# The state space branch by blocks of eight tokens: three matrices for each channel tile and a scan over 64 blocks

## The chip, the core and the metric

The kernel runs on one core of a Trainium2 chip. The metric is the time that the device measures for one execution, in microseconds (us). TensorE (PE in the rows) multiplies matrices and writes PSUM. VectorE (DVE), ScalarE (ACT) and GpSimd (POOL) work on tiles of 128 partitions. SyncE (SP) issues the DMAs of this kernel, in the order in which they stand in its queue. Every engine works through its own queue in order; an instruction that waits holds up those behind it.

## The reference, cut to what matters

The program is two layers of a first block (convolution, latent attention, a recurrent branch) and one layer of a second block. The second block has a differential attention with 8 heads, a state space branch (S5) over 1024 channels, and a merge of both. S5 has 64 groups of 16 channels, each group with 64 complex states; 512 tokens go through it one after the other:

```python
def s5_branch(u, lam_re, lam_im, log_dt, b_re, b_im, c_re, c_im, d_skip, w_glu, b_glu):
    ...
    mag = jnp.exp(lr * dt)
    ab_re = mag * jnp.cos(li * dt)
    ab_im = mag * jnp.sin(li * dt)
    ...
    bu_re = jnp.einsum('bsgc,gpc->bsgp', uf, bb_re)
    bu_im = jnp.einsum('bsgc,gpc->bsgp', uf, bb_im)
    ...
    _, _, xs_re, xs_im = lax.associative_scan(combine, (a_re, a_im, bu_re, bu_im), axis=1)
    y = (jnp.einsum('bsgp,gcp->bsgc', xs_re, c_re.astype(f32))
         - jnp.einsum('bsgp,gcp->bsgc', xs_im, c_im.astype(f32)))
    y = y.reshape(bsz, seq, D_SSM) + d_skip.astype(f32) * u.astype(f32)
    y = jax.nn.gelu(y.astype(u.dtype))
    return y * jax.nn.sigmoid(y @ w_glu + b_glu)
```

So the state is x(t) = a x(t-1) + B u(t) with a complex a per state, and the output is Re(C x(t)) + d u(t).

## The kernel before

Activations lie with 128 channels on the partitions and 512 tokens along the row. Each large product with a weight is made of three matmuls over 128x512 (`mm3`, lines 184 to 186: high by high, high by low, low by high parts). A weight comes in as 128 x 1024 raw values (`load_w`, line 159), ScalarE rounds it to the high part (line 169), VectorE subtracts for the low part (line 170). There are two raw buffers and three buffers each of high and low parts.

The second block runs over eight turns q = 0 to 7 (`second_block`). A turn does channel tile q of S5 (`ssm_u`, then `ssm_tile`), head q of the attention's scores (`diff_scores`), head q-1 of its values (`diff_values`) and a gate; its six input projections are 6 x 48 = 288 of the three-part matmuls. I call such a turn a head.

In `ssm_tile` four pairs of groups (128 complex states each) follow one another. Two matmuls give B u (line 1527). Four VectorE products with a cosine and a sine table (1529 to 1533) and two GpSimd sums (1531, 1534) turn every token's input back by its angle, so that two real scans over 512 tokens with the decay alone (1536, 1537) give the states; three VectorE products, two VectorE sums and two GpSimd products (1538 to 1543) turn them forward again; eight matmuls with C, 32 output columns each (1551), close the tile. The tables are read from DRAM (`CS`, 512 KB for a pair).

The tables are made in the output projections of layers 0 and 1 of the first block. `out_proj` runs over 16 column tiles c; after each it takes one more piece of a generator `k.prep`: first `ssm_prep` (parameters, B and C matrices), then `rotations` (32 tables; 10 in layer 0 and 22 in layer 1). In layer 1 `out_proj` also keeps three weighted sums on VectorE (1156, 1158) and two on GpSimd (1153, 1154).

The order of each engine's queue is set by a scheduler that simulates the program as written; weight loads have a high priority. Line numbers of the changed kernel are smaller by one to three in the unchanged part.

## Time and profile before

| what | value |
|---|---|
| median of 3 runs | 3424.55 us (3423.64 to 3424.78) |
| the profiled execution, and its span | 3426.18 us, span 3424.4 us |
| TensorE busy | 3306.3 us (97%) |
| VectorE busy | 1995.6 us (58%) |
| ScalarE, GpSimd busy | 1191.6 us (35%), 860.8 us (25%) |
| mean granted clock of TensorE | 0.981 |

The span is divided by the profile into 40 slices of 85.6 us; counted from 1: slices 24 to 31 are heads, slices 21 and 22 lie in the output projection of layer 1. Busy time of TensorE counts a matmul from its start to its modelled end, and matmuls overlap, so a busy share near 1 doesn't say that TensorE issues as fast as it can. How many matmuls start in a stretch says more.

### The profile page before, as it was taken

The page shows a single profiled execution, that of the slowest core. Times are in us where ns is not written, and L with a number is a line of the kernel's source. Part 1 is how long each engine was busy: PE and PEld are TensorE (multiplying, and loading weights), DVE is VectorE, ACT ScalarE, POOL GpSimd, SP SyncE. Part 2 cuts the span into 40 slices and gives each one's busy share as a digit, 9 for nine tenths or more (in the row PEclk, how much of TensorE's full clock was granted, in tenths as well). Part 3 has the DMA queues.
Part 4 walks back from the last instruction along what each step waited for, and adds up shares of the span by engine and source line. Part 5 has one row for each costly group of instructions (what it writes and reads, how often), then busy time and mean ns, then how long its engine had stood idle before and what let it go on. Part 6 is the DMA issues. An engine that isn't in the chain of part 4 may idle for free.

```text
span 3424.4 us, 41918 instructions
## 1 busy us (share of the span) xinstructions
PE 3306.3 (97%) x15603; PEld 2666.6 (78%) x15603; DVE 1995.6 (58%) x3035; ACT 1191.6 (35%) x1950; POOL 860.8 (25%) x978
## 2 busy tenths in 40 slices
...
DVE  4546635655754367455589689888888533232432
...
GB/s 173 153 174 139 130 129 151 123 102 152 200 145 126 159 153 136 136 152 110 96 176 221 95 139 116 116 122 122 116 122 110 222 107 100 108 103 103 154 143 113
DMA packets 687936, 466.27 MB, mean 136 GB/s; under 512 B 91286, under 2 KB 621995, under 8 KB 687731
## 3 DMA queue, kind: packets, MB, share of 16 engines
...
q8 instruction: 123, 2.02, 0.3%
q14 instruction: 83, 0.67, 0.1%
...
## 4 chain that ended last, share of the span: by engine, by line
PE 38%; DVE 10%; issue 3%; DMA 1%; ACT 1%; POOL 1%; SPq 0%; DVEq 0%; POOLq 0%; ACTq 0%
PE acc L185 10%; PE acc L186 10%; PE acc L184 10%; PE ps_b L186 2%; PE ps_b L185 2%; PE ps_b L184 2%; DVE wl L170 2%; DVE s L1536 1%; DVE x L1540 1%; DVE x L1541 1%; PE ps_s L1551 1%; DVE x L1537 1%; DVE b L1158 1%; DVE x L1538 1%; PE ps_s L930 1%
## 5 line engine op out<-in xcount | busy, mean ns | idle before, releaser
L186 PE MATMUL acc<-xh,wl 128*128 128x512 f32 x3552 | 1409.6, 397 | 15.8 <-DVE wl L170 15.7
L184 PE MATMUL acc<-xh,wh 128*128 128x512 f32 x3552 | 1404.6, 397 | 17.4 <-ACT c L772 5.0
L185 PE MATMUL acc<-xl,wh 128*128 128x512 f32 x3552 | 1410.3, 397 | 1.9 <-DVE xl L177 1.9
L170 DVE TENSOR_TENSOR wl<-wr,wh 128x1024 fp32r<-128x1024 f32 (+1 forms) x508 | 673.8, 1327 | 795.9 <-ACT wh L169 771.7
L169 ACT CAST wh<-wr 128x1024 fp32r<-128x1024 f32 (+1 forms) x508 | 529.6, 1043 | 1490.6 <-PE acc L185 1177.9
L184 PEld LDWEIGHTS acc<-xh,wh 128*128 128x128 f32 x3552 | 675.6, 190 | 171.1 <-issue 12.6
L186 PEld LDWEIGHTS acc<-xh,wl 128*128 128x128 f32 x3552 | 675.2, 190 | 168.0 <-DVE wl L170 20.6
L185 PEld LDWEIGHTS acc<-xl,wh 128*128 128x128 f32 x3552 | 675.8, 190 | 161.8 <-issue 18.0
L1745 POOL TENSOR_TENSOR b<-b,b 128x512 f32<-128x512 f32 x16 | 20.9, 1305 | 496.2 <-DVE b L1743 496.2
L1531 POOL TENSOR_TENSOR s<-s,s 128x512 f32<-128x512 f32 x32 | 45.2, 1413 | 243.0 <-DVE s L1530 237.5
L1743 DVE SCALAR_TENSOR_TENSOR b<-b,ps_b 128x512 f32<-128x512 f32 x32 | 22.0, 687 | 106.2 <-PE ps_b L186 106.2
L1153 POOL TENSOR_TENSOR b<-b,b 128x512 f32<-128x512 f32 x28 | 46.6, 1666 | 112.8 <-DVE b L1136 98.1
L1551 PE MATMUL ps_s<-x,s 128*32 128x512 f32 x128 | 47.0, 681 | 27.3 <-DVE x L1540 27.2
L1539 POOL TENSOR_TENSOR s<-s,x 128x512 f32<-128x512 f32 x32 | 52.0, 1625 | 82.1 <-DVE x L1537 57.7
L397 POOL TENSOR_TENSOR rr_a<-rv_a,mhalf 128x8 f32<-128x8 f32 (+1 forms) x24 | 46.5, 1939 | 103.2 <-DVE rv_a L392 103.2
L1473 POOL TENSOR_TENSOR r<-r,r 128x512 f32<-128x512 f32 x32 | 55.8, 1746 | 63.0 <-DVE r L1472 61.0
L598 DVE TENSOR_TENSOR pk<-pk,pk 128x224 f32<-128x224 f32 (+59 forms) x126 | 67.5, 536 | 3.4
L960 POOL TENSOR_TENSOR v<-v,c 128x512 f32<-128x512 f32 x16 | 20.6, 1289 | 184.2 <-ACT v L957 184.1
L599 DVE TENSOR_TENSOR pk<-pk,pk 128x224 f32<-128x224 f32 (+59 forms) x126 | 62.3, 495 | 3.5
L563 DVE TENSOR_TENSOR pk<-ps_m,mrk 128x512 f32<-128x512 f32 x32 | 22.1, 690 | 68.9 <-PE ps_m L560 68.9
L655 POOL COPY zm_pk<-pk 64x128 f32<-64x128 f32 x64 | 28.7, 449 | 131.1 <-DMA pk<-pack 130.9
L1763 POOL TENSOR_TENSOR b<-b,ln 128x512 f32<-128x512 f32 x16 | 20.7, 1292 | 152.2 <-DVE b L1762 125.7
...
## 6 DMA issues: line engine op xcount, KB each, us to landing
...
```

The costliest lines, as they stand in the source:

```text
L169: nc.scalar.copy(hi[:, : m * n], raw[:, : m * n])
L170: nc.vector.tensor_tensor(out=lo[:, : m * n], in0=raw[:, : m * n], in1=hi.bitcast(F32)[:, : m * n], op=ALU.subtract)
L184: self.nc.tensor.matmul(out, lhsT=wh, rhs=xh, start=st, stop=False)
L185: self.nc.tensor.matmul(out, lhsT=wh, rhs=xl, start=False, stop=False)
L186: self.nc.tensor.matmul(out, lhsT=wl, rhs=xh, start=False, stop=sp)
L397: nc.gpsimd.tensor_tensor(out=r.rearrange(flat), in0=v.rearrange(flat), in1=k.mhalf[:, 0:n], op=ALU.pow)
L598: eng.tensor_tensor(out=t3, in0=X[:, 0:n, c - 1 : c].to_broadcast([P, n, w]), in1=q[:, q.shape[1] - w :].unsqueeze(1).to_broadcast([P, n, ...
L599: eng.tensor_tensor(out=X[:, 0:n, c:], in0=X[:, 0:n, c:], in1=t3, op=A)
L1153: nc.gpsimd.tensor_tensor(out=sums[0], in0=sums[0], in1=t, op=ALU.add)
L1473: nc.gpsimd.tensor_tensor(out=x, in0=x, in1=m, op=SB)
L1539: G.tensor_tensor(out=t1, in0=sn, in1=t2, op=M)
L1551: nc.tensor.matmul(py[o], lhsT=lc[:, d, o], rhs=xs[p][d], start=(d == 0), stop=(d == 1))
```

## The change

The branch now works on blocks of eight tokens. For each channel tile of 128 channels `ssm_prep` builds three matrices of 128 x 1024 and one table, all kept in DRAM: `LB` (the eight inputs of a block to its last state, powers of a included), `LC` (the state before a block to its eight outputs), `TP` (the eight inputs of a block to its eight outputs directly, with d on the diagonal), and `CS` (cosine, sine and decay of 64 blocks for four pairs of groups). `turns` makes angles, `product` one complex product as two VectorE instructions and one on GpSimd. `rotations` and `times` are gone.

`ssm_u` writes the projected u to DRAM in the order (s, b), token in block by block, and reads it back with channel and s on the partitions: one write and eight reads of 16 x 8 rows of 256 bytes. `ssm_states` does 16 matmuls over 64 blocks, turns them with two products and two sums, scans the 64 blocks of four pairs, real and imaginary part in one instruction of 512, and turns back with two products and two sums. `ssm_tile` does 8 matmuls with `TP` and 16 with `LC`, then the gelu, and writes it to DRAM in eight pieces. The second block calls `ssm_states` ahead of `diff_scores` and `ssm_tile` behind it. `ssm_glu` takes the factor one half into its constants and puts the tokens in order again.

```diff
-        k.prep = chain(ssm_prep(k, a), rotations(k))
+        k.prep = ssm_prep(k, a)
...
-        times(k)
...
+    def turns(f, r, t, cos, sin):
+        x, m, y = k.b(), k.b(), k.b()
+        x3, y3 = (v.rearrange("p (a b) -> p a b", b=t.shape[2]) for v in (x, y))
+        V.tensor_tensor(out=x3, in0=f, in1=t, op=M)
+        G.tensor_tensor(out=y3, in0=r, in1=t, op=M)
+        V.tensor_scalar(out=m, in0=x, scalar1=MAGIC, scalar2=-MAGIC, op0=A, op1=A)
+        V.tensor_tensor(out=x, in0=x, in1=m, op=SB)
+        V.tensor_tensor(out=x, in0=x, in1=y, op=A)
+        V.tensor_scalar(out=m, in0=x, scalar1=MAGIC, scalar2=-MAGIC, op0=A, op1=A)
+        V.tensor_tensor(out=x, in0=x, in1=m, op=SB)
+        nc.scalar.activation(out=m, in_=x, func=AF.Abs)
+        nc.scalar.activation(out=cos, in_=m, func=AF.Sin, scale=-SIN2PI, bias=k.hpi)
+        nc.scalar.activation(out=sin, in_=x, func=AF.Sin, scale=SIN2PI)
...
+    turns(bc_last(fh, 16), bc_last(rl, 16), tb, co, si)
+    for q, t in enumerate((co, si)):
+        V.tensor_tensor(out=t, in0=t, in1=e.rearrange("p a b -> p (a b)"), op=M)
+        nc.sync.dma_start(out=PW[:, q], in_=t)
...
+    for j in range(4):
+        f, r, m8 = (keep[:, q, 8 * j : 8 * j + 8] for q in range(3))
+        o, d0 = k.b4((P, 2, S)), k.b((P, 8, NB))
+        turns(bc_last(f, NB), bc_last(r, NB), t8, o[:, 0], o[:, 1])
+        G.tensor_copy(out=d0, in_=bc_last(m8, NB))
+        G.memset(d0[:, :, 0:1], 0.0)
+        for i in range(2):
+            dst = k.CS[2 * j + i].rearrange("p d r b -> p d (r b)")
+            nc.sync.dma_start(out=dst[:, 0:2], in_=o[:, :, 256 * i : 256 * i + 256])
+            for d in (2, 3):
+                nc.sync.dma_start(out=dst[:, d], in_=d0[:, 4 * i : 4 * i + 4].rearrange("p r b -> p (r b)"))
+        yield
...
+    def product(o, x, y, op):
+        t = k.b((P, 4, TB, 16))
+        V.tensor_tensor(out=o, in0=x[0], in1=y[0], op=M)
+        G.tensor_tensor(out=t, in0=x[1], in1=y[1], op=M)
+        V.tensor_tensor(out=o, in0=o, in1=t, op=op)
...
+    for ct in range(8):
+        rows, prs = slice(ct * P, ct * P + P), slice(4 * ct, 4 * ct + 4)
+        c2, pw, bb = k.b((P, 2, 2, 64)), k.b((P, 2, 4, 16)), k.b((P, 2, 4, 16))
+        for q, key in enumerate(("ssm_c_re_2", "ssm_c_im_2")):
+            for d in range(2):
+                nc.sync.dma_start(out=c2[:, q, d], in_=a[key][0].rearrange("g c p -> (g c) p")[rows])
+        nc.sync.dma_start(out=pw, in_=PW[:, :, prs])
+        nc.sync.dma_start(out=bb, in_=BB[:, :, prs])
+
+        ps, lcm, CT = k.ps((P, 2, P)), k.b((P, 2, P)), k.b((P, 2, 4, 16))
+        for q in range(2):
+            nc.tensor.transpose(ps[:, q], c2[:, q].rearrange("p d w -> p (d w)"), k.ident)
+            V.scalar_tensor_tensor(out=lcm[:, q], in0=ps[:, q], scalar=(1.0, -1.0)[q], in1=cm, op0=M, op1=M)
+        lv = lcm.rearrange("p d (r g c) -> p d r g c", g=2, c=16)
+        G.tensor_tensor(out=CT, in0=lv[:, :, :, 0], in1=lv[:, :, :, 1], op=A)
...
+        lc = k.b4((P, 4, 2, P))
+        lc5 = lc.rearrange("p r d (s c) -> p r d s c", c=16)
+        product(lc5[:, :, 0], (wide(CT, 0), wide(CT, 1)), (power(0, 0), power(1, 0)), A)
+        product(lc5[:, :, 1], (wide(CT, 1), wide(CT, 0)), (power(0, 0), power(1, 0)), SB)
+        nc.sync.dma_start(out=k.LC[ct], in_=lc.rearrange("p r d m -> p (r d m)"))
+        yield
+        B = k.b4((P, 4, 2, P))
+        B5 = B.rearrange("p r d (s c) -> p r d s c", c=16)
+        product(B5[:, :, 0], (wide(bb, 0), wide(bb, 1)), (power(0, TB), power(1, TB)), SB)
+        product(B5[:, :, 1], (wide(bb, 0), wide(bb, 1)), (power(1, TB), power(0, TB)), A)
+        pk, kx = k.ps(), k.b((P, 240))
+        for d in range(2):
+            for r in range(4):
+                o = slice(32 * r, 32 * r + 32)
+                nc.tensor.matmul(pk[o, 0:P], lhsT=lcm[:, d, o], rhs=B[:, r, d], start=(d == 0), stop=(d == 1))
+
+        G.memset(kx[:, P:240], 0.0)
+        V.tensor_copy(kx[:, 0:112], pk[:, 0:112])
+        V.scalar_tensor_tensor(out=kx[:, 112:128], in0=m16, scalar=k.par2("d", ct), in1=pk[:, 112:128], op0=M, op1=A)
+        lb = k.b4((P, 4, 2, P))
         for h in range(2):
+            ps = k.ps((P, 2, 2, P))
+            for r in range(2):
+                for d in range(2):
+                    nc.tensor.transpose(ps[:, r, d], B[:, 2 * h + r, d], k.ident)
+            nc.scalar.copy(lb[:, 2 * h : 2 * h + 2], ps)
+        nc.sync.dma_start(out=k.LB[ct], in_=lb.rearrange("p r d m -> p (r d m)"))
+        tp = k.b4((P, 8, TB, 16))
+        for h in range(2):
+            ps = k.ps((P, 4, P))
+            for s in range(4):
+                c0 = 16 * (7 - 4 * h - s)
+                nc.tensor.transpose(ps[:, s], kx[:, c0 : c0 + P], k.ident)
+            nc.scalar.copy(tp[:, :, 4 * h : 4 * h + 4].rearrange("p g s c -> p s g c"), ps.rearrange("p s (g c) -> p s g c", c=16))
+        nc.sync.dma_start(out=k.TP[ct], in_=tp.rearrange("p g s c -> p (g s c)"))
         yield
...
-def rotations(k: K):
...
+def ssm_u(k: K, ct, x, w, pu=None):
+    nc = k.nc
+    u, ub = k.b(), k.b()
+    pu = pu or k.inproj(x, [(w[:, C2_U + ct * P : C2_U + ct * P + P], 0)])
+    nc.scalar.copy(u.rearrange("p (s b) -> p b s", s=TB), pu.rearrange("p (b s) -> p b s", s=TB))
+    du = k.dp.tile([8, 16, TB, NB], F32, name=k.nm("du"))
+    nc.sync.dma_start(out=du.rearrange("g c s b -> (g c) (s b)"), in_=u)
+    for s in range(TB):
+        nc.sync.dma_start(out=ub[16 * s : 16 * s + 16].rearrange("c (g b) -> c g b", b=NB), in_=du[:, :, s].rearrange("g c b -> c g b"))
+    mats = []
+    for src in (k.LB, k.CS, k.TP, k.LC):
+        t = k.b4((P, 1024))
+        nc.sync.dma_start(out=t, in_=src[ct] if len(src.shape) == 3 else src[ct].rearrange("p d r b -> p (d r b)"))
+        mats.append(t)
+    return ub, *mats
...
+def ssm_states(k: K, ub, lb, cs, tp, lc):
...
+    lb, cs = lb.rearrange("p (r d m) -> p r d m", d=2, m=P), cs.rearrange("p (d n) -> p d n", d=4)
+    pb = k.ps((P, 2, 4, NB))
+    for r in range(4):
+        for d in range(2):
+            for g in range(2):
+                o, g0 = slice(64 * g, 64 * g + 64), (2 * r + g) * NB
+                nc.tensor.matmul(pb[o, d, r], lhsT=lb[:, r, d, o], rhs=ub[:, g0 : g0 + NB], start=True, stop=True)
+    pb = pb.rearrange("p d r b -> p d (r b)")
+    c, sn = (cs[:, q : q + 1].to_broadcast([P, 2, 256]) for q in range(2))
+    t1, t2, z = (k.b((P, 2, 256)) for _ in range(3))
+    V.tensor_tensor(out=t1, in0=c, in1=pb, op=M)
+    V.tensor_tensor(out=t2, in0=sn, in1=pb, op=M)
+    V.tensor_tensor(out=z[:, 0], in0=t1[:, 0], in1=t2[:, 1], op=A)
+    V.tensor_tensor(out=z[:, 1], in0=t1[:, 1], in1=t2[:, 0], op=SB)
+    z2 = z.rearrange("p d n -> p (d n)")
+    V.tensor_tensor_scan(out=z2, data0=cs[:, 2:4].rearrange("p d n -> p (d n)"), data1=z2, initial=0.0, op0=M, op1=A)
+    V.tensor_tensor(out=t1, in0=c, in1=z, op=M)
+    V.tensor_tensor(out=t2, in0=sn, in1=z, op=M)
+    xs = k.b((P, 2, 4, NB))
+    x3 = xs.rearrange("p d r b -> p d (r b)")
+    V.tensor_tensor(out=x3[:, 0], in0=t1[:, 0], in1=t2[:, 1], op=SB)
+    V.tensor_tensor(out=x3[:, 1], in0=t1[:, 1], in1=t2[:, 0], op=A)
+    return xs
...
+def ssm_tile(k: K, ct, xs, ub, lb, cs, tp, lc, out):
...
-    if True:
-        lc = k.b((P, 2, P))
-        nc.sync.dma_start(out=lc, in_=k.LC[ct])
-        xs = []
-        for q in range(4):
-            s = 4 * ct + q
...
+    py = [k.ps((P, 4, NB)) for _ in range(2)]
+    for r in range(4):
+        for g in range(2):
+            g0 = (2 * r + g) * NB
+            nc.tensor.matmul(py[g][:, r], lhsT=tp[:, 2 * r + g], rhs=ub[:, g0 : g0 + NB], start=(r == 0), stop=False)
+    for r in range(4):
+        for d in range(2):
+            for g in range(2):
+                o = slice(64 * g, 64 * g + 64)
+                nc.tensor.matmul(py[g][:, r, 1:NB], lhsT=lc[o, r, d], rhs=xs[o, d, r, 0 : NB - 1], start=False, stop=(r == 3 and d == 1))
...
+    V.scalar_tensor_tensor(out=t, in0=t, scalar=1.0, in1=v, op0=A, op1=M)
+    dy = k.dp.tile([8, 16, TB, NB], F32, name=k.nm("dy"))
+    for s in range(TB):
+        nc.sync.dma_start(out=dy[:, :, s].rearrange("g c b -> c g b"), in_=t[16 * s : 16 * s + 16].rearrange("c (g b) -> c g b", b=NB))
+    out.t[ct] = dy.rearrange("g c s b -> (g c) (s b)")
...
-        nc.scalar.activation(out=th, in_=ps, func=AF.Tanh, scale=0.5, bias=k.par2("b_glu", ct))
+        nc.scalar.activation(out=th, in_=ps, func=AF.Tanh, scale=0.25, bias=k.par2("b_glu", ct))
         V.scalar_tensor_tensor(out=th, in0=th, scalar=1.0, in1=src.get(ct), op0=A, op1=M)
         o = k.b()
-        V.scalar_tensor_tensor(out=o, in0=th, scalar=0.25, in1=sz.get(ct), op0=M, op1=M)
+        o3, sz3 = (t.rearrange("p (b s) -> p b s", s=TB) for t in (o, sz.get(ct)))
+        V.scalar_tensor_tensor(out=o3, in0=th.rearrange("p (s b) -> p b s", s=TB), scalar=0.125, in1=sz3, op0=M, op1=M)
         out[ct] = o
...
-    with k.phase("qs", {"s": 3}, s=SS, x=SX, s4=S4, u=2):
+    with k.phase("qs", {"s": 3}, s=SS, s4=S4):
...
         u = ssm_u(k, 0, x, w, first[0])
         for q in range(8):
-            ssm_tile(k, q, *u, ys)
+            xs = ssm_states(k, *u)
             with k.use("a", "a"):
                 nxt = diff_scores(k, q, x, w, first[1:] if q == 0 else [], lows[q % 2])
+            ssm_tile(k, q, xs, *u, ys)
             if q < 7:
                 u = ssm_u(k, q + 1, x, w)
             with k.use("a", "a"):
```

Three places in the queues follow. The first is VectorE in a head between two weight tiles (`wl`), before: the piece around the third and fourth pair of groups; `s` and `x` are tiles of the branch, `mag` the decay, `ps_s` the product B u.

```order
L1536 SCALAR_TENSOR_TENSOR s_16623<-mag,s_16623 128x512
L1537 SCALAR_TENSOR_TENSOR x_16625<-mag,x_16625 128x512
L1543 TENSOR_TENSOR x_16601<-x_16601,s_16599 128x512
L170 TENSOR_TENSOR wl_17077<-wr_17075,wh_17076 128x1024
L1538 TENSOR_TENSOR x_16626<-s_3302_16617,s_16623 128x512
L1529 TENSOR_TENSOR s_16647<-s_3309_16641,ps_s_16643 128x512
L1530 TENSOR_TENSOR s_16648<-s_3309_16641,ps_s_16644 128x512
L1532 TENSOR_TENSOR x_16649<-s_3309_16641,ps_s_16644 128x512
L1533 TENSOR_TENSOR x_16650<-s_3309_16641,ps_s_16643 128x512
```

And of the change, the same place in a head: everything that the branch does on VectorE for its states.

```order
L409 SCALAR_TENSOR_TENSOR s_17305<-s_17303,acc_17254 128x512
L1592 TENSOR_TENSOR s_17326<-s_3457_17236,ps_s_17309 128x512
L1593 TENSOR_TENSOR s_17327<-s_3457_17236,ps_s_17309 128x512
L1594 TENSOR_TENSOR s_17328<-s_17326,s_17327 128x256
L1595 TENSOR_TENSOR s_17328<-s_17326,s_17327 128x256
L1597 SCALAR_TENSOR_TENSOR s_17328<-s_3457_17236,s_17328 128x512
L1598 TENSOR_TENSOR s_17326<-s_3457_17236,s_17328 128x512
L1599 TENSOR_TENSOR s_17327<-s_3457_17236,s_17328 128x512
L1602 TENSOR_TENSOR s_17336<-s_17326,s_17327 128x256
L1603 TENSOR_TENSOR s_17336<-s_17326,s_17327 128x256
L169 TENSOR_TENSOR wl_17425<-wr_17423,wh_17424 128x1024
```

Ten instructions for each of four pairs became nine for the whole tile, four of them half as long; they stand in one piece behind a gate and ahead of the weights.

The second place is SP's queue where a tile's u is put in place: before from SBUF to SBUF in twelve pieces (`us`), with a weight load `wr` ahead of them.

```order
L159 DMA wr_19505<-in_w_in_dram 128x8x128
L1504 DMA us_s_19116<-s_19121 32x512
L1504 DMA us_s_19116<-s_19122 32x512
L1504 DMA us_s_19116<-s_19121 32x512 x2
L1504 DMA us_s_19116<-s_19122 32x512
```

Of the change: eight writes of the gelu (`dy`), a weight, the write of u (`du`), a weight, the eight reads of it, and the next weight.

```order
L1635 DMA dy_18437<-s_18431 16x8x64 x8
L158 DMA wr_18654<-in_w_in_dram 128x8x128
L1563 DMA du_18510<-s_18446 128x512
L158 DMA wr_18745<-in_w_in_dram 128x8x128
L1565 DMA s_18447<-du_18510 16x8x64 x8
L158 DMA wr_18751<-in_w_in_dram 128x8x128
L158 DMA wr_18823<-in_w_in_dram 128x8x128
```

The reads of `du` wait until its write has landed, and the weight behind them waits with them.

The third place is VectorE in the output projection of layer 1, before: two tables of `rotations` (1470 to 1472) between the sums `b` of one column tile.

```order
L1136 SCALAR_TENSOR_TENSOR b_15576<-b_15574,acc_15525 128x512
L1470 SCALAR_TENSOR_TENSOR r_15487<-r_14628,fh,r_15488 128x512
L1158 SCALAR_TENSOR_TENSOR b_14655<-b_15576,wz_b_14631,b_14655 128x512
L1158 SCALAR_TENSOR_TENSOR b_14656<-b_15576,wz_b_14631,b_14656 128x512
L1471 SCALAR_TENSOR_TENSOR r_15487<-r_14628,rl_7249,r_15487 128x512
L170 TENSOR_TENSOR wl_15702<-wr_15700,wh_15701 128x1024
L1472 TENSOR_SCALAR r_15488<-r_15487 128x512
L1156 SCALAR_TENSOR_TENSOR b_14658<-b_15580,wz_b_14631,b_14658 128x512
L1470 SCALAR_TENSOR_TENSOR r_15500<-r_14628,fh,r_15501 128x512
L1471 SCALAR_TENSOR_TENSOR r_15500<-r_14628,rl_7249,r_15500 128x512
L1472 TENSOR_SCALAR r_15501<-r_15500 128x512
```

Of the change: the four complex products of one channel tile (1488, 1490) between the sums.

```order
L169 TENSOR_TENSOR wl_15934<-wr_15932,wh_15933 128x1024
L1153 SCALAR_TENSOR_TENSOR b_14704<-b_15774,wz_b_14677,b_14704 128x512
L1504 SCALAR_TENSOR_TENSOR r_15566<-ps_r_15565,cm 128x128
L1488 TENSOR_TENSOR r_3093_15573<-r_15567,r_15557 128x4x128 x2
L1488 TENSOR_TENSOR r_3107_15657<-r_15558,r_15557 128x4x128 x2
L1490 TENSOR_TENSOR r_3093_15573<-r_3093_15573,r_15574 128x4x128
L1490 TENSOR_TENSOR r_3093_15573<-r_3093_15573,r_15578 128x4x128
L1490 TENSOR_TENSOR r_3107_15657<-r_3107_15657,r_15658 128x4x128
L169 TENSOR_TENSOR wl_15940<-wr_15938,wh_15939 128x1024
L1490 TENSOR_TENSOR r_3107_15657<-r_3107_15657,r_15662 128x4x128
```

Three instructions for a pair of groups became eight for four pairs, each of 512 elements and each second one behind a product on GpSimd. TensorE's queue in the same stage has new rows, here between the matmuls of one column tile:

```order
L184 MATMUL acc_16169<-xl_14658,wh_16164 128x512
L1528 MATMUL ps_r_15891<-r_3149_15882,r_15791 32x128 x8
L1538 MATMUL ps_r_15905<-ident,r_3149_15882 128x128 x4
L185 MATMUL acc_16169<-xh_14657,wl_16165 128x512
L183 MATMUL acc_16169<-xh_14663,wh_16164 128x512
```

The 8 small matmuls and the transposes wait for `B` from VectorE, and the matmuls of the projection (`acc`) stand behind them.

## Rows read from the trace of the kernel before

**Rows 1.** The page, part 2: VectorE's busy tenths in 40 slices of the span

```profile
DVE  4546635655754367455589689888888533232432
```

**Rows 2.** Stretches: us, then busy (count) of PE PEld DVE ACT POOL; clock, DMA

```profile
2124.30:2567.20 442.90, 423.89 (x1944) 328.54 (x1943) 369.06 (x575) 154.02 (x297) 166.05 (x105) 0.98 0.40 119
...
1410.00:1690.00 280.00, 279.95 (x1549) 232.56 (x1548) 150.90 (x314) 112.38 (x230) 50.33 (x86) 1.00 0.40 122
2800.00:3000.00 200.00, 200.00 (x879) 164.54 (x878) 59.88 (x49) 43.79 (x48) 16.58 (x12) 1.00 0.36 104
...
1738.00:1880.00 142.00, 124.49 (x503) 98.69 (x502) 133.41 (x133) 96.77 (x144) 78.41 (x47) 0.94 0.60 198
...
784.00:955.00 171.00, 169.09 (x776) 139.78 (x776) 105.68 (x147) 76.30 (x109) 65.92 (x42) 1.00 0.62 178
```

**Rows 3.** Chain of work that ended last: start us, us, what; whole span

```profile
2124.29 1.06 ACT wh L169
...
2567.24 1.06 ACT wh L169
```

**Rows 4.** TensorE by line, 2124.3 to 2567.2: count, busy, mean ns, idle before

```profile
L186 PE MATMUL acc<-xh,wl 128*128 128x512 f32 x481 | 191.7, 399 | 0.0
L184 PE MATMUL acc<-xh,wh 128*128 128x512 f32 x480 | 191.3, 399 | 0.0
...
L1551 PE MATMUL ps_s<-x,s 128*32 128x512 f32 x80 | 29.0, 663 | 16.3 <-DVE x L1540 16.3
...
L1527 PE MATMUL ps_s<-us_s,s 96*128 96x512 f32 x40 | 14.3, 409 | 2.7 <-DVE x L1532 2.7
```

**Rows 5.** The chain again: a run of L1551, a run of attention matmuls

```profile
2260.72 0.99 PE ps_s L1551 x8
...
2663.55 1.11 PE ps_a L1669 x10
```

**Rows 6.** Stretches of 10 us within one head, columns as in rows 2

```profile
2236.00:2246.00 10.00, 10.00 (x43) 6.58 (x42) 10.00 (x12) 2.02 (x3) 5.93 (x5) 1.00 0.55 153
2246.00:2256.00 10.00, 6.21 (x21) 4.04 (x21) 10.00 (x10) 1.56 (x2) 8.51 (x6) 0.80 0.40 122
2256.00:2266.00 10.00, 10.00 (x39) 6.19 (x38) 7.22 (x12) 1.68 (x2) 3.45 (x3) 0.86 0.35 107
```

**Rows 7.** VectorE by line, 2124.3 to 2567.2, columns as in rows 4

```profile
L1536 DVE TENSOR_TENSOR_SCAN s<-mag,s 128x512 f32<-128x512 f32 x20 | 36.2, 1811 | 0.0
...
L1538 DVE TENSOR_TENSOR x<-s,s 128x512 f32<-128x512 f32 x20 | 13.7, 687 | 0.0
...
L1529 DVE TENSOR_TENSOR s<-s,ps_s 128x512 f32<-128x512 f32 x20 | 13.4, 671 | 0.0
```

**Rows 8.** TensorE by line, whole span: matmuls near the new ones in shape

```profile
L560 PE MATMUL ps_m<-pk 64*128 64x128 f32 x256 | 22.9, 297 | 2.1 <-DVE pk L551 1.3 <-DVE pk L563 0.8
...
L673 PE MATMUL ps_m<-tk_pk,zm_pk 128*128 128x64 f32 x128 | 16.7, 268 | 0.0
...
L721 PE MATMUL ps_s<-gv_pk,pk 128*64 128x64 f32 x256 | 15.3, 224 | 0.0
```

**Rows 9.** VectorE by line, 1738 to 1880, columns as in rows 4

```profile
L1158 DVE SCALAR_TENSOR_TENSOR b<-b,wz_b,b 128x512 f32<-128x512 f32 x22 | 35.7, 1661 | 0.1
...
L1471 DVE SCALAR_TENSOR_TENSOR r<-r,rl,r 128x512 f32<-128x512 f32 x22 | 24.0, 1094 | 0.4
L1470 DVE SCALAR_TENSOR_TENSOR r<-r,fh,r 128x512 f32<-128x512 f32 x22 | 20.8, 951 | 1.3 <-ACT r L1469 1.3
L1472 DVE TENSOR_SCALAR r<-r 128x512 f32<-128x512 f32 x22 | 11.4, 520 | 0.3
```

**Rows 10.** Chain, whole span: landings of DMAs between SBUF and DRAM

```profile
1712.84 4.08 DMA c<-mix
...
1853.14 6.75 DMA CS<-r
```

**Rows 11.** Instructions in order of time on SP: start us, us, line, count

```profile
2368.20 6.70 SPq L1504 DMA_DIRECT2D us_s<-s  x9
```

More of the change, by code (lines that the diff above doesn't have):

```diff
@@ L2 @@
 from contextlib import ExitStack, contextmanager, nullcontext
-from itertools import chain
 import concourse.bass as bass
@@ L1089, in out_proj @@
     nc = k.nc
-    with k.use("r"):
-        times(k)
     last = l == DEPTH - 1
@@ L1282 @@
 NST = 32
+TB, NB = 8, 64
 def second_params(k: K, a):
@@ L1342, in turn @@
         return t[:, 0:NST]
[L1345 to L1346 removed]
+    cm = k.lp.tile([P, P], F32, name="cm")
+    G.memset(cm, 0.0)
     for g in range(2):
[L1348 to L1350 removed]
+        G.memset(cm[g * 64 : g * 64 + 64].rearrange("p (s g c) -> p s g c", g=2, c=16)[:, :, g], 1.0)
+    m16 = k.lp.tile([P, 16], F32, name="m16")
+    V.tensor_reduce(out=m16, in_=k.ident.rearrange("p (g c) -> p c g", c=16), op=ALU.add, axis=AX)
     lr = cols(a["ssm_lambda_re_2"][0].rearrange("(s g) p -> s (g p)", g=2))
@@ new lines, in ssm_prep @@
+    G.tensor_tensor(out=e, in0=bc_last(lrdt, 16), in1=tb, op=M)
+    nc.scalar.activation(out=e, in_=e, func=AF.Exp)
+    turns(bc_last(fh, 16), bc_last(rl, 16), tb, co, si)
+    for q, t in enumerate((co, si)):
+        V.tensor_tensor(out=t, in0=t, in1=e.rearrange("p a b -> p (a b)"), op=M)
+        nc.sync.dma_start(out=PW[:, q], in_=t)
+    keep = k.small((P, 3, NST), "keep", 1)
+    for q, t in enumerate((fh, rl, e[:, :, TB - 1])):
+        V.tensor_copy(keep[:, q], t)
+    k.CS = k.dp.tile([8, P, 4, 4, NB], F32, name="CS")
```

175 lines of the change are left out of this document (47 added, 128 removed).

## The prediction, made before the changed kernel was run

> **What bounds the kernel now.** I read the page first, then stretches by engine, then the chain of waits, then groups by line inside the stretches that the change touches. The page's slices show VectorE nearly full in two places: slices 21 and 22, the output projection of layer 1, and slices 24 to 31, the heads of the second block [rows 1]. Where VectorE is light, TensorE starts its matmuls back to back: 200 us hold 879 starts, so one three-part matmul costs 200 / 879 = 0.2275 us [rows 2]. That is the price to measure a stretch by.
>
> A head repeats exactly: the chain passes line 169 at 2124.29 and again, five heads on, at 2567.24, so one head takes 442.95 / 5 = 88.6 us [rows 3]. What TensorE needs in those five: 1441 three-part matmuls at 0.2275 make 327.8 us [rows 4]; 80 records of line 1551, eight of which took 0.99 us in one run, make 9.9 [rows 4, 5]; 40 of line 1527, with 512 columns too, make 9.1 [rows 4]; the other 383 of the 1944 records, attention, at 1.11 / 10 us make 42.5 [rows 2, 5]. The sum is 389.3, or 77.9 a head. So 10.7 us of a head are lost to something else, although TensorE counts as busy for 423.9 of 442.9 us [rows 2].
>
> The loss has a place. In 30 us of one head 43 + 21 + 39 = 103 matmuls start where 132 would fit, VectorE is at 10 of 10 us in the first two thirds, and the clock is granted at 0.80 and 0.86 in the last two, behind the standstill [rows 6]. TensorE stands before line 1551 until line 1540 on VectorE has made the states, and before 1527 for the products that free its PSUM: 16.3 and 2.7 us in five heads [rows 4]. The rest is thin issue around these stops. VectorE is the bound of the first half of a head, TensorE of the second.
>
> **The heads, part by part.** What goes on VectorE: ten groups of 20 instructions in five tiles, from line 1536 (36.2 us) down to 1529 (13.4), 191.9 us together, 38.4 a head [rows 7]. What comes: two products from PSUM at 0.67, two of 512 from SBUF and four of 256, and one scan at 1.81. The SBUF ones cost 0.69 as line 1538 shows, or 1.66 as line 1158 shows beside a busy GpSimd; a 256 wide one half of that [rows 7, 9]. That is 5.9 to 9.8; I take 6.5, since the four GpSimd products and sums of each pair go too. VectorE then has 369.1 / 5 - 38.4 + 6.5 = 41.9 us of work a head [rows 2], 52% of 81 us. The nearest stretch with attention on such a share is 1410 to 1690: VectorE 150.9 of 280 us, TensorE 279.95 [rows 2]. I take it that TensorE will be the bound of the whole head.
>
> So the question is what TensorE gains or loses. Gone are 16 x 0.124 + 8 x 0.2275 = 3.8 us. New are 16 matmuls into 64 output columns, 8 into 128 and 16 over 64 rows, all with 63 or 64 moving columns. Full fp32 matmuls stand twice in the trace (80 records of 1551 for five tiles of eight), so 32, 16 and 32 records. The nearest shapes: line 721 at 15.3 / 256 = 0.060 us, line 673 at 16.7 / 128 = 0.130, line 560 at 22.9 / 256 = 0.089 [rows 8]. That makes 1.9 + 2.1 + 2.9 = 6.9 as the dear end. Line 560 moves 128 columns, the new ones 63; at half price, and with a quarter off the first kind for pairs that overlap, it is 5.0. I take 6.2, nearer to the rows as they are. The head's need becomes 77.9 - 3.8 + 6.2 = 80.3, and TensorE pays 2.4 us for being relieved of VectorE.
>
> Waits that the change adds: the first state matmul needs u to be written to DRAM and read back. A landing took 4.08 to 6.75 us [rows 10] and nine small issues on SP 6.70 us, 0.74 each [rows 11]: write, eight issues, read are 14.1 to 19.4 us. In the changed queue 96 three-part matmuls stand between the last one for u and that matmul, 21.8 us, from the third tile on; so it is covered. For the second tile there are 51, 11.6 us, and the first tile's `LC` matmuls follow its states by 32, 7.3 us against VectorE's 6.5. These two may cost 5 to 8 us, once. Behind the wait stands the whole queue of TensorE. For the other heads 144 matmuls, 32.8 us, stand between the states' matmuls and those that use them. I add 0.7 us a head for all this: 81.0.
>
> A head saves 88.6 - 81.0 = 7.6 us. The first head starts on projections made earlier and the last runs into the next stage, so I count 7.5 heads: 57 us. With the ends 5.0 and 6.9 and waits of 0 to 2 us a head this is 47 to 66.
>
> **The tables.** In layer 1's output projection VectorE is the bound over most of its length: 133.4 of 142 us, while TensorE starts 503 matmuls, 114 us of work [rows 2]. Rotations are 24.0 + 20.8 + 11.4 = 56.2 us of that [rows 9]. Six channel tiles replace them, with eight products of 512 each, two 128 wide and two tiny ones. A product costs between 0.67 (line 1529) and 1.66 (line 1158) [rows 7, 9]; the rotations' own two, with the same GpSimd load beside them, averaged 1.02 [rows 9]. So 8 x 1.02 and 1.1 for the rest are 9.3 a tile and 56 for six: nothing gained. The ends are 39 and 86. TensorE gets 6 x about 3 us (18 transposes at 0.111, 16 small records at the price of line 721), 18 us, into 28 us of room. Its matmuls stand in order behind `B`, but VectorE is late anyway; I count 0, between -17 and +15, since not all of 30 us dearer products would be late in a stage whose last fifth has VectorE half idle [rows 1].
>
> In layer 0 TensorE is the bound, 169.1 of 171 us with VectorE at 105.7 [rows 2]. Two tiles add 5 to 6 us of TensorE's work and 32 transposes of the old matrices, 3.6 us, go: +2.5. The angle work there hides under VectorE's 65 idle us. The gate and the reordering in `ssm_glu` are eight instructions in a stage that has VectorE at 3 tenths [rows 1]: 0.
>
> The sum: -57 + 2.5 = -54.5. The profiled execution took 3426.18 us, 1.6 above the median of 3424.55, and 1.8 above its own span; the differences are the same for all. 3424.55 - 54.5 gives 3370.
>
> **Rivals.** First, SP's queue takes VectorE's place. The weight behind `du` waits for its landing and eight issues, 4.1 to 6.75 and 5.9 us, and then lands itself in 4.1 or more: 14.1 to 18.7 us without a new weight. One weight tile feeds 24 matmuls, 5.5 us, and two ready ones beside the one in use, with two raw ones behind them, last 11 to 22 us. For it: TensorE will be faster at eating them than now. Against it: twelve issues of `us` stand in that queue today [rows 11] and no weight is late for it in a head. If only 11 us are in stock, a head loses about 5 us: 7.5 x 5 = 38, so 3408.
> The trace of before has no row for the landing of a DRAM write in rows of 256 bytes, which `dy` now is. The Trainium skill (DMA: Bandwidth & Descriptors, Specifications) says that below 512 bytes a transfer is a read-modify-write and off line rate; by that rule such a landing would be longer than rows 10, and if it were longer by one more 4.08 us in every head that would be 31 us and 3401. No run here shows it yet, and no term above rests on it.
>
> Second, the tables get cheaper: without the chain through ScalarE the products run at 0.69, VectorE saves 17 us and TensorE, with 28 us of room, takes them: 3353. Against it: GpSimd has as many products as before.
>
> Third, slower: each channel tile passes four 1024 wide tiles through two buffers of the tag `r4`, each buffer waiting for a landing twice. Products 6 us, transposes and copies 3, two landings up to 13.5: 22.5 us, in two column tiles of 142 / 11 = 12.9 us [rows 2, 9], 25.8. VectorE's queue holds the next product until a landing is in, and with it the low parts of all weights. It costs eight times what lies over 25.8; from 33 us a tile on the change is slower. At 36 us it is 8 x 10.2 = 82, so 3452. Against it: today's tables pass through the same two buffers.
>
> Fourth, nothing gained: the attention's own chain sets the head once the branch is gone, at 88 us. Against it stands 1410 to 1690. About 3425.
>
> **How the numbers follow.** The forecast has 0.60, the late weights 0.16, the cheaper tables 0.14, the slower tables 0.06, no gain 0.04. The forecast's own bounds give 3345 to 3395; the range goes down to 3342 for part of the cheaper tables and up to 3408 for the middle of the late weights. Faster by over 0.2% (7 us, about what a measurement of this kernel can tell from no change): 0.60 + 0.16 + 0.14 = 0.90; within 0.04; slower 0.06.
>
> **What would show it.** Right: a head of 80 to 82 us; TensorE's starts in a 10 us stretch at 43 or more everywhere in a head; VectorE near 42 us a head; no idle of TensorE before the state matmuls beyond the second tile. The new matmuls between 5 and 7 us a head show the price right or wrong. The layer 1 projection should end within 15 us of the same place. Idle before three-part matmuls put down to line 169's or 170's successors in the heads means the first rival; VectorE idle behind a landing in the projection means the third. What would make the prediction wrong above all is a price of the small matmuls well over 7 us, since 7.5 heads carry it.

## The result, and the profile after

The changed kernel takes 3366.44 us (median; 3364.86 to 3367.76) against 3424.45 (3423.64 to 3424.78): a ratio of 0.9829, 95% interval 0.9816 to 0.9843. The forecast was 3370, within 3342 to 3408. The total came out 4 us from the forecast, but two of its terms missed by 20 and by 9 us, in opposite directions; most of what follows is about these two.

The page of the changed kernel, busy time and VectorE's slices, to be held against [rows 1]:

```profile
PE 3284.4 (98%) x16291; PEld 2688.8 (80%) x16291; DVE 1740.7 (52%) x2783; ACT 1123.9 (33%) x1842; POOL 661.4 (20%) x879
...
DVE  4546644655864448535668865444445522322432
```

No slice has VectorE above 8 tenths now, and the heads stand at 4 and 5 tenths. Its stretches (columns as in [rows 2]): six heads, those 10 us of one head in which the fewest matmuls start, and the output projections of layer 0 and layer 1.

```profile
2089.90:2571.30 481.40, 481.40 (x2654) 405.55 (x2653) 231.97 (x487) 187.28 (x361) 39.76 (x30) 1.00 0.38 113
...
2182.20:2192.20 10.00, 10.00 (x47) 8.23 (x47) 7.60 (x17) 5.69 (x11) 0.00 (x0) 1.00 0.29 76
...
800.00:971.00 171.00, 162.57 (x754) 130.62 (x752) 119.51 (x156) 56.13 (x76) 75.18 (x61) 0.99 0.55 161
...
1748.40:1941.90 193.50, 181.57 (x925) 145.78 (x924) 161.06 (x167) 52.26 (x68) 93.79 (x69) 0.98 0.55 172
```

In the heads TensorE is busy for all of 481.40 us at the full 2.4 GHz (granted 1.00), where it had 423.9 of 442.9 at 0.98; VectorE has 38.7 us a head. The chain of the changed kernel, one head from its first attention matmuls on, with the new matmuls (1617 `TP`, 1622 `LC`, 1588 `LB`), and the same place five heads later:

```profile
2142.15 0.79 PE ps_a L366 x8
...
2159.85 1.28 PE ps_s L1617 x12
...
2161.58 0.39 PE ps_s L1617 x4
2161.97 1.93 PE ps_s L1622 x32
...
2201.86 0.26 PE ps_s L1588 x2
...
2203.53 1.08 PE ps_s L1588 x30
...
2543.28 0.79 PE ps_a L366 x8
```

(2543.28 - 2142.15) / 5 = 80.2 us a head, after 88.6 [rows 3]. To see where the whole 58 us come from, I counted the three-part matmuls; both kernels have 12,000 of them, in stages of the same length. When the n-th one starts:

| n | place | before | after | difference |
|---|---|---|---|---|
| 2500 | start of layer 0's projection | 781.1 | 784.5 | +3.4 |
| 3300 | behind it | 993.4 | 1008.7 | +15.2 |
| 5700 | start of layer 1's projection | 1719.5 | 1735.5 | +16.0 |
| 6600 | second block begins | 1988.2 | 2007.4 | +19.2 |
| 6928 | 1.1 heads on | 2103.4 | 2100.1 | -3.3 |
| 8656 | six heads on | 2634.8 | 2581.4 | -53.4 |
| 8800 | half a head on | 2678.2 | 2620.1 | -58.1 |
| 11700 | near the end | 3347.2 | 3288.8 | -58.3 |

So layer 0's projection costs 11.8 us, layer 1's 3.2, and the second block gains 77.3. The first 3.4 us lie in stages whose code is the same; these move by as much from one kernel to the next below (at n = 2400 they stand -4.3 to +0.8 from this one), so I explain nothing by them. Layer 0's projection itself differs by up to 2.1 us between kernels whose code is the same there.

### The profile page after: what moved, and what is told of

Read it like the earlier page. It is cut to its first block, busy times and chain, and to the rows that moved or that the text cites. A ratio compares the mean times of both kernels' runs of the same rounds, so it can differ in the third digit from the quotient of the medians.

```text
span 3366.0 us, 42736 instructions
## 1 busy us (share of the span) xinstructions
PE 3284.4 (98%) x16291; PEld 2688.8 (80%) x16291; DVE 1740.7 (52%) x2783; ACT 1123.9 (33%) x1842; POOL 661.4 (20%) x879
## 5 line engine op out<-in xcount | busy, mean ns | idle before, releaser
L169 DVE TENSOR_TENSOR wl<-wr,wh 128x1024 fp32r<-128x1024 f32 (+1 forms) x508 | 665.3, 1310 | 919.1 <-ACT wh L168 907.5
L396 POOL TENSOR_TENSOR rr_a<-rv_a,mhalf 128x8 f32<-128x8 f32 (+1 forms) x24 | 36.9, 1538 | 516.3 <-DVE rv_a L391 516.3
L818 ACT ACTIVATE a<-ps_a,nm_a,sp_a 128x128 f32<-128x128 f32 (+3 forms) x64 | 39.2, 615 | 49.5 <-DVE nm_a L815 48.1
L183 PE MATMUL acc<-n,wh 128*128 128x512 f32 x128 | 52.5, 410 | 0.0
L184 PE MATMUL acc<-n,wh 128*128 128x512 f32 x128 | 51.4, 401 | 0.0
L183 PE MATMUL ps_b<-ya,wh 128*128 128x512 f32 x128 | 50.7, 396 | 0.0
L184 PE MATMUL ps_b<-ya,wh 128*128 128x512 f32 x128 | 50.6, 396 | 0.0
```

What stands on the lines that cost most here:

```text
L169: nc.vector.tensor_tensor(out=lo[:, : m * n], in0=raw[:, : m * n], in1=hi.bitcast(F32)[:, : m * n], op=ALU.subtract)
L183: self.nc.tensor.matmul(out, lhsT=wh, rhs=xh, start=st, stop=False)
L184: self.nc.tensor.matmul(out, lhsT=wh, rhs=xl, start=False, stop=False)
L396: nc.gpsimd.tensor_tensor(out=r.rearrange(flat), in0=v.rearrange(flat), in1=k.mhalf[:, 0:n], op=ALU.pow)
L818: nc.scalar.activation(out=pr[:, 0:n], in_=ps[:, 0:n], func=AF.Exp, scale=scale, bias=nm, accum_out=sm)
```

## The experiments

### Was VectorE the bound of a head before?

The kernel before, the turning back left out:

```diff
-            V.tensor_tensor(out=t3, in0=c, in1=t0, op=M)
-            G.tensor_tensor(out=t1, in0=sn, in1=t2, op=M)
-            V.tensor_tensor(out=t3, in0=t3, in1=t1, op=SB)
...
-            xs.append((t3, t2))
+            xs.append((t0, t2))
```

> The kernel before, with the turning back of the states left out (four VectorE products and sums and two GpSimd products for each pair of groups); the matmuls take the scans' results as they are. That is 4 x 4 x 0.69 = 11 us of VectorE's work less in a head, of 73.8, and not one matmul less. If VectorE is the bound of the first half of a head, a head falls from 88.6 us towards TensorE's need of 77.9, say to 79 to 82, and the kernel by 8 x 6.6 to 9.6 = 53 to 77 us, to 3348 to 3372. If the attention's own chain or TensorE's small matmuls hold the head, the gain is below 15 us.

3358.2 us (ratio to before 0.9802, 0.9787 to 0.9818), 65 us less. Its chain, two marks four heads apart, and the stretch:

```profile
2220.98 0.79 PE ps_a L367 x8
...
2546.72 0.79 PE ps_a L367 x8
```

```profile
2133.00:2539.00 406.00, 406.00 (x1930) 323.59 (x1923) 284.63 (x496) 153.87 (x295) 87.51 (x65) 1.00 0.43 127
```

A head takes 325.7 / 4 = 81.4 us, and TensorE is busy throughout, with every matmul of the kernel before still there. So the branch's elementwise work held the head; the attention's chain (fourth rival) didn't. The edit also takes away the two GpSimd products of a pair, so by itself it doesn't part VectorE's load from the waits beside GpSimd; that VectorE was full where TensorE starved stands in [rows 6].

### Is TensorE the bound now, and what do the small matmuls cost?

The changed kernel with the VectorE chain of the states four times over, and, apart from that, with the small matmuls twice:

```diff
+    for _ in range(4):
         V.tensor_tensor(out=t1, in0=c, in1=pb, op=M)
...
+    for _ in range(2):
         for r in range(4):
...
                 nc.tensor.matmul(pb[o, d, r], lhsT=lb[:, r, d, o], rhs=ub[:, g0 : g0 + NB], start=True, stop=True)
```

> The changed kernel with the VectorE chain of the states (nine instructions, 5.65 us by their means) made four times over: +17 us of VectorE in a head, 38.7 to 55.7 of 80.2. If TensorE alone sets the head, and 144 matmuls (32.8 us) cover the chain, which becomes 22.6 us long, the time stays within 5 us of 3366. If VectorE's chain is on the path, up to 8 x 17 = 136 us are added.

> The changed kernel with all matmuls of LB, TP and LC made twice. In the trace of the changed kernel they take 1.08, 1.71 and 1.93 us in one run, 4.7 a head. If TensorE sets the head, 8 x 4.7 = 38 us are added: 3404; at the 6.2 of my prediction it would be 50: 3416. If TensorE had room, less than 10.

The first: 3375.3 us, 9 more, where I had allowed 5. Two marks of its chain five heads apart, and the stretch between them:

```profile
2152.08 0.79 PE ps_a L366 x8
...
2553.22 0.79 PE ps_a L366 x8
```

```profile
2152.08:2553.22 401.14, 401.14 (x2214) 337.92 (x2212) 267.38 (x541) 155.85 (x301) 33.69 (x25) 1.00 0.39 115
```

A head still takes 401.1 / 5 = 80.2 us with VectorE at 53.5. By the count of matmuls all of the loss (+10) lies in the first turn, between n = 6600 and 6928; there TensorE waited 5.9 us in one place, behind ScalarE's copy of the next u. So the cover that I had named holds in seven heads and not in the first.

The second: 3416.2 us (3413.7 to 3420.6), 50 more, the value for 6.2 us a head. Its chain:

```profile
2149.81 0.79 PE ps_a L366 x8
...
2582.11 0.79 PE ps_a L366 x8
```

A head takes 432.3 / 5 = 86.5 us, 6.2 more. TensorE is the bound: what it is given is paid in full. In the changed kernel the rows above sum to 1.67 + 1.93 + 1.34 = 4.9 us; the doubled ones cost 1.3 more than that, in part between the attention's matmuls that the order puts among them.

### What do the tables cost, and on which engine?

Tables for one channel tile only; and, with all tiles, half of each complex product:

```diff
-    for ct in range(8):
+    for ct in range(1):
...
-        t = k.b((P, 4, TB, 16))
         V.tensor_tensor(out=o, in0=x[0], in1=y[0], op=M)
-        G.tensor_tensor(out=t, in0=x[1], in1=y[1], op=M)
-        V.tensor_tensor(out=o, in0=o, in1=t, op=op)
```

> The changed kernel with LB, LC and TP made for the first channel tile only, and read by all eight; CS is made in full. It says what seven tiles of tables cost in the two output projections. In layer 1 the fifteen column tiles need 720 x 0.2275 = 164 us of TensorE, six channel tiles of tables 18 more, and 193.5 were taken, so 12 are lost in waits for VectorE. If all that is freed, layer 1 gains 26 to 30; the one tile in layer 0 gains 3 to 7: 3329 to 3337. If the tables are free, as my prediction had them but for 2.5 us, the time stays above 3360.

> The changed kernel with half of every complex product of the tables left out: the GpSimd product and the VectorE sum (32 of each kind: 8 in layer 0, 24 in layer 1). TensorE's work on the tables stays whole. It parts the 37 us that seven channel tiles cost by the run with one tile. If layer 1 loses 18 us to TensorE's own small matmuls (720 starts and these make 181.5 of its 193.5 us) and 12 to a late VectorE, the 12 go, and 2 to 4 in layer 0: 3350 to 3353. If VectorE is not late and TensorE's share is everything, the time stays within 4 us of 3366.

One tile: 3331.4 us, 35.0 less; by the count of matmuls 30.8 of it in layer 1 (n = 5700 to 6600) and 4.5 in layer 0 (2500 to 3300). Half products: 3349.7, 16.8 less; 12.8 in layer 1 and 1.0 in layer 0, the latter within the 2.1 us by which that stage differs anyway. Layer 1's projection, of the run with one tile and of the one with half products:

```profile
1742.00:1905.00 163.00, 163.00 (x726) 135.31 (x724) 107.17 (x93) 39.65 (x47) 52.35 (x33) 0.98 0.48 144
```

```profile
1741.00:1922.00 181.00, 180.28 (x936) 147.29 (x934) 126.63 (x141) 53.17 (x71) 55.67 (x45) 0.99 0.61 189
```

TensorE is full in both. So layer 1 pays 18 us for TensorE's own work on six tiles, as counted, and 12.8 for a VectorE that is late. Of TensorE's waits there (1745 to 1950) only 0.4 us are for low parts of weights; 9.5 are before the small matmuls that need the products (total, times, longest):

```profile
PE ps_r L1528 <- DVE r L1490: 9.5, 7, 2.4
```

The kernel before paid 27 there (720 starts need 164 of its 190.6 us), and the last run of the next section shows that nearly all of it was for a VectorE slowed by GpSimd. So the room of 28 us was used up, not left over.

### Why is VectorE late: GpSimd beside it

In layer 0 TensorE waited for both parts of the weights (rows of the waits in the changed kernel, 785 to 1010: total, times, longest), where before it had waited 1.0 us for low parts and none for high ones:

```profile
PE acc L185 <- DVE wl L169: 3.4, 6, 1.2
PE acc L183 <- ACT wh L168: 3.3, 2, 2.8
```

The longest of these, 2.8 us, ends near 870. In order of time, ScalarE, then VectorE and GpSimd there (start, us, line; in brackets the idle time before it and what ended it):

```profile
860.35 0.62 ACT L1443 ACTIVATE r<-r 128x512 f32<-128x512 f32 x1
867.93 0.63 ACT L1441 ACTIVATE r<-r 128x512 f32<-128x512 f32 x1 [6.97 <-DVE r L1440]
868.47 0.61 ACT L1443 ACTIVATE r<-r 128x512 f32<-128x512 f32 x1
868.99 1.03 ACT L168 CAST wh<-wr 128x1024 fp32r<-128x1024 f32 x1
```

```profile
858.79 1.78 DVE L1434 TENSOR_TENSOR r<-keep_r,t_r 128x512 f32<-128x512 f32 x1
...
861.95 1.51 DVE L1436 TENSOR_SCALAR r<-r 128x512 f32<-128x512 f32 x1
...
864.39 1.53 DVE L1437 TENSOR_TENSOR r<-r,r 128x512 f32<-128x512 f32 x1
866.02 0.69 DVE L1438 TENSOR_TENSOR r<-r,r 128x512 f32<-128x512 f32 x1
866.75 0.43 DVE L1439 TENSOR_SCALAR r<-r 128x512 f32<-128x512 f32 x1
```

```profile
857.88 2.14 POOL L1150 TENSOR_TENSOR b<-b,b 128x512 f32<-128x512 f32 x1 [5.35 <-DVE b L1133]
859.98 1.49 POOL L1435 TENSOR_TENSOR r<-keep_r,t_r 128x512 f32<-128x512 f32 x1
861.43 1.74 POOL L1151 TENSOR_TENSOR b<-b,b 128x512 f32<-128x512 f32 x1
...
864.04 1.32 POOL L1435 TENSOR_TENSOR r<-keep_r,t_r 128x512 f32<-128x512 f32 x1
```

While GpSimd worked, VectorE took 1.5 to 1.8 us for products and sums that take 0.69 once it was done, and 1.51 for what takes 0.43. ScalarE stood 7 us before the angle, with the rounding of the next weight behind it in its queue, and TensorE stood 2.8 us for that weight. Over both projections, a VectorE product of lines 1488 and 1490 took 0.68 us with GpSimd idle, and 1.54 to 1.78 with GpSimd busy throughout. The order of starts decides it: each of the 35 that took over 1 us began while a GpSimd instruction was under way and ended 0.55 us after that one. Of the other 29, nine had a GpSimd instruction start 0.04 to 0.16 us behind them and still took 0.68 to 0.69, one had a GpSimd memset under way and took 0.68, and beside the rest GpSimd was idle.

The Trainium skill (SBUF — State Buffer, SBUF: two separate sides) says why: the two engines share one pair of ports, and whichever starts first, a GpSimd instruction or one of VectorE in a two-port mode or with two inputs from SBUF (the latter only against a GpSimd instruction that reads SBUF), holds the pair until it ends, while the other waits. The trace agrees: 0.68 against 1.54 to 1.78 by the order of starts, the memset that cost nothing, and no such difference for an instruction that reads PSUM (last section).

Three kernels take GpSimd's work away from VectorE's side, by making it on VectorE: the tables' products; those, the angles' products and the copies of the decays (these on ScalarE); and the products, angles and the two running sums of the projections.

```diff
-        G.tensor_tensor(out=t, in0=x[1], in1=y[1], op=M)
+        V.tensor_tensor(out=t, in0=x[1], in1=y[1], op=M)
...
-        G.tensor_tensor(out=y3, in0=r, in1=t, op=M)
+        V.tensor_tensor(out=y3, in0=r, in1=t, op=M)
...
-            nc.gpsimd.tensor_tensor(out=sums[0], in0=sums[0], in1=t, op=ALU.add)
-            nc.gpsimd.tensor_tensor(out=sums[nz], in0=sums[nz], in1=sq, op=ALU.add)
+            nc.vector.tensor_tensor(out=sums[0], in0=sums[0], in1=t, op=ALU.add)
+            nc.vector.tensor_tensor(out=sums[nz], in0=sums[nz], in1=sq, op=ALU.add)
```

> The changed kernel with the GpSimd product of each complex product made on VectorE. In the projections of the changed kernel a VectorE product of two SBUF tiles took 0.68 us with GpSimd idle and 1.54 to 1.78 with GpSimd busy all through it. If GpSimd beside it is what makes the products dear, three at 0.68 (2.04) replace two at 1.38 + 0.95 (2.33), and layer 1 has some 7 to 13 us of VectorE less: 3358 to 3364. If it is VectorE's number of instructions that counts, 24 x 0.68 = 16 us come on top: 3375 or more.

> As a_vprod, with the angles' GpSimd products (five) on VectorE and the four GpSimd copies of the decays on ScalarE, all in layer 0. Layer 0 lost 12 us to the tables where I had counted 2.5; between 860.98 and 867.93 ScalarE stood before the angle (its absolute value) that VectorE had not made, with the weights' rounding behind it, and VectorE's five instructions before it took 1.5 to 1.8 us beside a busy GpSimd. If that is the loss, 2 to 5 us less than a_vprod; if the order alone does it, no difference.

> As the run before, and the two running sums of both output projections and the angle products on VectorE too, so that GpSimd stands beside nothing there. Layer 1's VectorE would have 30 low parts at 1.21, 28 weighted sums at 0.74, 72 products at 0.68, 28 sums at 0.69 and some 30 us more: 156 us, against 161 measured: about as a_vprod or some us dearer, 3358 to 3372. If the GpSimd sums are the larger part of the trouble, 3352 or less.

They took 3357.1, 3355.0 (3349.4 to 3357.5) and 3343.0 us (3342.8 to 3345.9). More instructions on VectorE didn't make it slower. The first is 9 us below the changed kernel, though its ratio (0.9804, 0.9789 to 0.9819) just touches the change's. The second isn't told apart from the first; in their two profiled executions its layer 0 projection is 4.7 us shorter. The third is clear of both and went past the 3352 that I had set for the case in which the GpSimd sums are the larger part: its ratio to before is 0.9764 (0.9750 to 0.9779), below the change's 0.9829 (0.9816 to 0.9843). VectorE in layer 1's projection, the changed kernel and the third one (count, busy, mean ns, idle before):

```profile
L169 DVE TENSOR_TENSOR wl<-wr,wh 128x1024 fp32r<-128x1024 f32 x30 | 47.5, 1587 | 5.8 <-ACT r L1539 3.1 <-ACT wh L168 1.6 <-issue 1.1
L1155 DVE SCALAR_TENSOR_TENSOR b<-b,wz_b,b 128x512 f32<-128x512 f32 x28 | 36.4, 1339 | 0.3
L1488 DVE TENSOR_TENSOR r<-r,r 128x512 f32<-128x512 f32 x24 | 31.7, 1376 | 2.3 <-POOL r L1506 2.3
L1490 DVE TENSOR_TENSOR r<-r,r 128x512 f32<-128x512 f32 x24 | 21.9, 950 | 0.0
```

```profile
L169 DVE TENSOR_TENSOR wl<-wr,wh 128x1024 fp32r<-128x1024 f32 x30 | 37.2, 1240 | 24.5 <-ACT wh L168 24.5
L1155 DVE SCALAR_TENSOR_TENSOR b<-b,wz_b,b 128x512 f32<-128x512 f32 x28 | 20.4, 746 | 0.0
L1488 DVE TENSOR_TENSOR r<-r,r 128x512 f32<-128x512 f32 x24 | 16.4, 686 | 0.6 <-POOL r L1506 0.6
L1489 DVE TENSOR_TENSOR r<-r,r 128x512 f32<-128x512 f32 x24 | 16.3, 686 | 0.0
L1490 DVE TENSOR_TENSOR r<-r,r 128x512 f32<-128x512 f32 x24 | 15.2, 685 | 0.0
```

The weights' low parts and the weighted sums, which no edit touches, lose 10 and 16 us; three products cost VectorE 48 us where two beside GpSimd cost it 54. By the count of matmuls the third kernel wins 9.4 us in layer 0 and in layer 1 13.8 up to n = 6300, of which 5.4 are given back at its end. Of the 11.8 us that layer 0 had lost, some 2.5 are left, what the prediction had for TensorE's own work there, as far as a stage can be read that varies by 2 us.

Is that a fault of the change? The same in the kernel before, with the rotations' subtraction:

```diff
-        nc.gpsimd.tensor_tensor(out=x, in0=x, in1=m, op=SB)
+        V.tensor_tensor(out=x, in0=x, in1=m, op=SB)
```

> The kernel before, with the two running sums of both output projections and the subtraction of each rotation table moved from GpSimd to VectorE; all else as before. Is the cost of GpSimd beside VectorE one of the change's tables, or did the kernel before pay it too? By the durations with an idle GpSimd, its layer 1 would have 160 us of VectorE where 168 were measured, and TensorE needs 164 of 190.6: 10 to 20 us less, 3405 to 3415. If only the new products suffer, the time stays within 4 us of 3425.

3404.5 us (ratio 0.9938, 0.9925 to 0.9950), 20 less. By the count of matmuls its profiled execution gains 25.5 us in layer 1 and 0.6 in layer 0. The weighted sums, which the edit doesn't touch, took 1661 ns in [rows 9] and here:

```profile
L1158 DVE SCALAR_TENSOR_TENSOR b<-b,wz_b,b 128x512 f32<-128x512 f32 x28 | 19.8, 740 | 0.0
```

So the kernel before paid nearly as much for it, in layer 1. With these on VectorE on both sides, the change is worth 3404.5 - 3343.0 = 61.5 us; with GpSimd on both sides it was 58.0, which the intervals don't tell apart.

### A faster version

The 5.4 us at the end of layer 1 stand before the products of the last channel tile, which are not ready when the last column tile is. A wait of TensorE in the third kernel:

```profile
PE ps_r L1528 <- DVE r L1490: 8.2, 1, 8.2
```

Two pieces of the tables are started earlier, in layer 1 or in layer 0:

```diff
                 next(k.prep, None)
+                if last and c in (1, 2):
+                    next(k.prep, None)
```

```diff
-                next(k.prep, None)
+                for _ in range(2 if not last and c in (1, 2) else 1):
+                    next(k.prep, None)
```

> The run with all of it on VectorE (3343), and two more pieces of the tables started behind the second and third column tile of layer 1, so that the last channel tile is done before the last column tile. There TensorE stood 8.2 us before the products of the last tile, and 5.5 us of what layer 1 had gained were lost. If they come back: 3336 to 3340. If the piece only moves the load to a place where VectorE is late, 3343 or more.

> The same run, with the two more pieces started early in layer 0, so that three channel tiles lie in layer 0 and five in layer 1. TensorE's 3 us for a tile move from one stage to the other; the end of layer 1 gains 5.5 as in the run before: 3336 to 3340. If VectorE in layer 0 becomes late between the fourth and the ninth column tile, where it was at 8 to 10 tenths, 3343 or more.

The first: 3345.4 us (3339.4 to 3348.7), no gain; that wait is gone and others came, 4.7 us before the last sum and 2.5 before a low part. The second: 3339.6 (3336.6 to 3341.2), ratio to before 0.9751 (0.9738 to 0.9765): the fastest here that still makes all the tables, faster than both kernels of the case. Its 3.4 us on the run without it are as expected, but the intervals of the two ratios overlap.

## Why the prediction was right, and where it wasn't

**The heads, mechanism: right.** VectorE was the bound of the first half [rows 6], and taking its work away moves a head to TensorE's need: the run without turning back shows the first of these, the run with the states four times over the second. VectorE has 38.7 us (forecast 41.9).

**The heads, size: nearly.** TensorE's need was put at 65.6 + 14.7 = 80.3 and is 66.5 + 13.7 = 80.2. The small matmuls took 4.9 us instead of 6.2, just under my low end, though their price at the margin, doubled, is 6.2; a three-part matmul took 0.231 instead of 0.2275. The 0.7 us of waits were not there: the waits of TensorE in 2142 to 2543 are empty. A head gains 8.4, not 7.6.

**The number of heads: the step that failed on the second block.** "I count 7.5 heads" gave 57, bounds 47 to 66; it is 77.3. (With the ends as the prediction names them, 5.0 and 6.9 and waits of 0 to 2, the bounds come to 42 and 71; 77.3 lies outside these too. The first rival's 14.1 to 18.7 us likewise: two landings of up to 6.75 and 5.9 of issues make up to 19.4.) From n = 6928 to 8656, six heads, 50.1 us are gained. The other 27.2 lie at the ends, for which I had counted 1.5 heads, 11.4 us. I had measured the loss in heads that repeat and not looked at the first ones, where the kernel before stood longest. Two stretches of it:

```profile
2009.00:2019.00 10.00, 6.11 (x18) 3.71 (x17) 10.00 (x12) 5.00 (x8) 4.60 (x4) 0.83 0.65 169
2069.00:2079.00 10.00, 6.09 (x25) 4.12 (x23) 10.00 (x8) 1.05 (x1) 10.00 (x6) 0.95 0.28 92
```

Eighteen and 25 matmuls started where 44 would fit, with VectorE full, below the 21 and 39 of [rows 6]. And the one-off cost of 5 to 8 us that I had put into the changed kernel's first tiles isn't there: TensorE waits 1.2 us in all from 1958 to 2142.

**Layer 1's tables: right by its bounds, for a mixed reason.** Forecast 0 (-17 to +15), measured +3.2. TensorE's 18 us were counted rightly, but no room took them up: they are paid in full. The sum came out near 0 because VectorE's lateness went from 27 to 12.8, and most of that is now the waiting of the small matmuls behind the products, which the prediction had put at nothing.

**Layer 0's tables: the step that failed.** "The angle work there hides under VectorE's 65 idle us": an average over 171 us. Forecast +2.5, measured +11.8. The work came in a lump (between 840 and 880 VectorE was busy for 36.8 of 40 us), slowed by GpSimd, and on ScalarE it stood in front of the weights. The share of a stage says nothing of the queue at one place. I had read 0.69 against 1.66 in [rows 7, 9] and taken an average of them as the price of a product; that average mixes two cases, with and without a GpSimd instruction under way, and the dear one holds for the low parts and sums beside the products as well.

**The rivals.** Late weights: no; TensorE waits for none in the heads. SP issued the write of u at 2178.09 and the first read of it at 2180.09, so the landing took under 2 us, not 4.1 to 6.75, and in five heads it held SP's queue for 4.4 us together:

```profile
2178.09 0.34 SPq L1563 DMA_DIRECT2D du<-s  x1
2178.96 0.38 SPq L158 DMA_DIRECT2D wr<-in_w_in_dram  x1
2180.09 4.33 SPq L1565 DMA_DIRECT2D s<-du  x8
```

The reads are issued by 2184.4, and the matmuls that need them start at 2201.86. The Trainium skill's rule on rows under 512 bytes (DMA: Bandwidth & Descriptors, Specifications) would have cost 31 us by my estimate, with one more 4.08 us in every head. The packets in the trace show no such time: in five heads the 10,240 packets of 256 bytes took 15 to 18 ns in the main, those of 512 bytes 27, and in this head the last of the eight writes of `dy` was issued at 2174.09 and its last packet ended at 2175.45. So the small packets are somewhat slower for each byte, and nothing waits for them. The tables' two-buffer chain (third rival): no wait of VectorE for a landing of such a tile in layer 1. Cheaper tables (second): not so in the changed kernel, but the reason given, products at 0.69, is what the runs on VectorE alone make true.

So 3370 was met because the second block gave 20 us more and layer 0 took 9 more, with 3 us more in layer 1 and some 4 in stages that weren't touched. The mechanism in the heads was right; that the total came within 4 us was luck, misses of opposite sign.
